# Deeper weight buffers for the last tile, gate stores on another queue, S5 outputs grouped by array tile

## The chip, the cores and the metric

The kernel runs as one program on one core of a Trainium2 chip. The metric is the device time of one execution in microseconds (us). Three runs of the kernel before took 1943.7, 1947.05 and 1947.4 us; the median, 1947.05, is the figure to compare with.

## The reference, cut to what matters

One layer for two groups of tokens: 512 prompt tokens, and 8 samples of 8 tokens. An S5 state-space mixer and an RWKV-7 mixer share one input projection; their outputs go through `w_out`, and then a product-key expert layer (PEER) follows: per token and head the 16 best of 128 x 128 experts.

```python
y = einsum(c_re, hs_re) - einsum(c_im, hs_im) + d_skip * u      # S5 outputs
x = x + ga1 * (concat([y_s5, y_rw]) @ w_out)
h = rmsnorm(x, norm2_g) * (1 + sc2) + sh2
q = (h @ w_q).reshape(T, 8, 2, 64)
s1, s2 = q[:, :, 0] @ keys1, q[:, :, 1] @ keys2                  # then top 16 of the pair sums
act = gelu(sum(u_tab[idx] * h))
ff = sum(gate * act * v_tab[idx])
y = rmsnorm(x + ga2 * ff, final_norm_g)
```

## The kernel before, in words

The 576 tokens are five tiles, taken in `ORDER = (1, 2, 3, 0, 4)`: tile 0 holds the 64 sample tokens, tiles 1 to 4 the prompt, 128 tokens each. Tiles 1, 2 and 3 are "dense": for them the expert layer runs as two full matrix products over all 16384 experts, in 128 blocks of 128 experts, with a table of gates that is zero for the experts not chosen. Tiles 0 and 4 gather their chosen rows instead.

**First part.** `phase1` makes the input projection; beside it `s5gen` computes the S5 group. Its outputs (lines 755 to 771) come for 4 quarters of 8 groups: per pair of groups `j` four matmuls of 64 rows (state against `CL`, real and imaginary part, the two halves `hf` of the array each into its own PSUM bank `pts[hf]`), and then two matmuls of 128 rows (`U` against `Tm`) that finish the pair's sums.

**Tile pipeline.** Five steps are woven, step `i` holding at most: `back` of the next tile and `front` of the one after (RWKV), `select` of tile `od[i]`, `pick` of tile `od[i-1]`, and `gbuild` of tile `od[i-2]`.
- `select` multiplies by `w_out` (line 1229, eight 512 KB loads `wo`), applies the modulation rows `ga`, `sh` and a norm, turns the result `h2` (line 1246) into `hT` (line 1257), multiplies by `w_q` (line 1269, eight 512 KB loads `wq`, one per head) and scores against `keys` (lines 1283 and 1285). All those loads go through one pool with two buffers (`tag="w", bufs=2`).
- `pick` finds the top 16 on VectorE, and for a dense tile leaves the chosen indices and gates in `dib` and `dix` (lines 1381 and 1382).
- `gbuild` makes the gate table of one dense tile in 32 groups of 4 tokens: VectorE makes a one-hot `oh` (line 1487); ScalarE (lines 1491, 1492) or VectorE (line 1494) makes `B`; ScalarE (line 1497) or GpSimd (line 1499) makes `A`; TensorE multiplies (line 1502); ScalarE copies into `Gst` (line 1503); every fourth group a 1 MB store `Gd<-Gst` leaves on SyncE's queue (line 1505). The tiles `ab` of `A` and `B` come from 9 buffers for the first two dense tiles, and for the third (`d == 2`) from a second pool `gp2` with 15.

In the last step (`i = 4`) only `select` of tile 4, `pick` of tile 0 and `gbuild` of tile 3 are left. `SO = {4: 4000}` gives that `select` a higher priority.

**Dense loop.** After the last `select`, 128 blocks: load 512 KB of `u_t` and of `v_tab`, split each into two parts (ScalarE line 1513, VectorE line 1514; lines 1615, 1616), first product `pd` (line 1517, 24 matmuls), Gelu, times the gates `Gr` (loaded back from `Gd` for 8 blocks at a time, line 1572), second product `po` (line 1620, 18 matmuls). `pick` of tile 4 and the 384 gathers of tiles 0 and 4 run beside it.

A scheduler orders each engine's instructions from a priority and a model of times; the order is fixed when the program is built. Every load or store of SyncE and ScalarE takes one of eight completion semaphores in turn, and its issue waits until the earlier transfer on that semaphore has landed.

Of the kernel before, what the change touches and what calls it, by code (L numbers as in the profile page):

```python
# [6 lines left out]
F32 = mybir.dt.float32  # L7
# [11 lines left out]
D = 1024  # L19
# [3 lines left out]
KB = 8  # L23
# [154 lines left out]
class Kernel:  # L178
# [4 lines left out]
    RATE = 3.0  # L183
    WS5, WAD, WS6, WA6, WD = 3.0, 0.0, 1.0, 1.0, 0.3
    PB = {"r": 3, "s": 3, "h": 1, "g": 1}
    UX, UWT, AB2 = 0, 0.5, 15
    UG = True
    UO = -100000
    PO, GO, SO, RO, FO = {}, {}, {4: 4000}, {}, {}
    FB = 32  # L190
    PW = 3.0
    B2 = {"r": 7, "l": 8, "b": 7, "s": 5}
# [451 lines left out]
    def s5gen(self, A):  # L644
        nc, I, O, vc, ident, p3 = self.nc, self.I, self.O, self.vc, self.ident, self.p5
        V, S, G, T, SY = nc.vector, nc.scalar, nc.gpsimd, nc.tensor, nc.sync
# [6 lines left out]
        U = p3.tile([128, 32, 72], F32, name="U", tag="U")  # L653
# [7 lines left out]
        for q in range(4):  # L661
            for r in range(2):
                pt = ps([128, 4, 72])
                for jj in range(4):
                    j = 4 * q + jj
# [20 lines left out]
        Tm = self.pB.tile([128, 32, 128], F32, name="Tm", tag="BTm")  # L686
# [72 lines left out]
        for q in range(4):  # L759
            pts = [ps([72, 4, 128]), ps([72, 4, 128])]  # L760
            for jj in range(4):
                j = 4 * q + jj
                for r in range(2):
                    for hf in range(2):
                        sl = slice(64 * hf, 64 * hf + 64)
                        T.matmul(pts[hf][:, jj, :], Hs[sl, r, j, 0:72], CL[sl, r, j, 1:9, :].rearrange("p a b -> p (a b)"),
                                 start=(r == 0), stop=False)
                for hf in range(2):
                    T.matmul(pts[hf][:, jj, :], U[:, 2 * j + hf, :], Tm[:, 2 * j + hf, :], start=False, stop=True)
            for hf in range(2):  # L770
                S.activation(Y[:, :, 8 * q + hf:8 * q + 8:2, :], pts[hf].rearrange("p g (t h) -> p t g h", h=16), AF.Gelu)
            yield
# [52 lines left out]
    def open_outer(self):  # L825
        o = self.so = Scope(self.tc)
        kw = dict(side="right", reuse_waits="tile")
        self.sm = o.pool("sm", 2, **kw)
        dn = o.pool("dn", **kw)
        self.dix = dn.tile([128, 2, 128 * len(self.DENSE)], F32, name="dix")  # L830
        io = dn.tile([128, 160], F32, name="iota")
        self.nc.sync.dma_start(io, self.I["iota"])
        self.dib = dn.tile([128, 128 * len(self.DENSE)], BF16, name="dib")
        self.io4 = dn.tile([128, 128, 4], BF16, name="io4")
        self.nc.gpsimd.tensor_copy(self.io4, io[:, :128, None].to_broadcast([128, 128, 4]))
        self.iota, self.off, self.wid = io[:, :128], io[:, 128:144], io[:, 144:160]
        m = self.sx = Scope(self.tc)
        wq = m.pool("wq", **kw)
        self.ws = m.pool("ws", **kw)
        self.t2p["s"] = m.pool("t2s", **kw)  # L840
        self.t4p["s"] = m.pool("t4s", **kw)
        self.sw = m.pool("sw", 1, **kw)
        self.G2 = wq.tile([128, D], F32, name="G2")
        g = self.sg = Scope(self.tc)
        self.gp = g.pool("gp", **kw)
        self.gs = g.pool("gs", self.GS, **kw)
# [354 lines left out]
    def select(self, ti):  # L1201
        yo = self.yo.pop(ti)
        nc, I, O = self.nc, self.I, self.O
        V, S, G, T, SY = nc.vector, nc.scalar, nc.gpsimd, nc.tensor, nc.sync
        t2, t4, ps, ident, sm = self.t2, self.t4, self.ps, self.ident, self.sm
        sw = self.sw
        smp = ti == 0
        dns = ti in self.DENSE
        c0 = 0 if smp else 64 + 128 * (ti - 1)
        ysd = t2([4, 128], "s")  # L1210
        if smp:
            SY.dma_start(ysd[:, :, 0:64], self.yd[:, :, 0:64])
            SY.dma_start(ysd[:, :, 64:128], self.yd[:, :, 0:64])
        else:
            SY.dma_start(ysd, self.yd[:, :, c0:c0 + 128])
        x1 = t4([D], "s")
        if smp:
            SY.dma_start(x1[0:64], I["x_all"][0:64, :])
            SY.dma_start(x1[64:128], I["x_all"][0:64, :])
        else:  # L1220
            SY.dma_start(x1, I["x_all"][c0:c0 + 128, :])
        tmp = t4([D], "s")
        lhs = [ysd[:, k, :] if k < 4 else yo[:, k - 4, :] for k in range(KB)]
        pos_ = [ps([128, 512], "s"), ps([128, 512], "s")]
        for k in range(KB):
            wo = self.ws.tile([128, D], F32, name="wo", tag="w", bufs=2)
            SY.dma_start(wo, I["w_out"][k * 128:(k + 1) * 128, :])
            for n in range(2):
                T.matmul(pos_[n], lhs[k], wo[:, n * 512:(n + 1) * 512], start=(k == 0), stop=(k == KB - 1))  # L1229
            if k % 2:  # L1230
                yield
        ga1 = self.ws.tile([128, D], F32, name="ga1", tag="w", bufs=2)
        self.mod(ga1, 0, smp)
        sh2 = self.ws.tile([128, D], F32, name="sh2", tag="w", bufs=2)
        self.mod(sh2, 1, smp)
        for n in range(2):
            V.tensor_tensor(tmp[:, n * 512:(n + 1) * 512], pos_[n], ga1[:, n * 512:(n + 1) * 512], op=OP.mult)
        V.tensor_tensor(x1, x1, tmp, op=OP.add)
        ss = sm.tile([128, 1], F32, name="ss")
        S.activation(tmp, x1, AF.Square, accum_out=ss)  # L1240
        self.rstd(ss, ss, 1e-6, 128, sm)
        SY.dma_start(self.x1d[ti], x1)
        yield
        h2 = t4([D], "s")
        V.scalar_tensor_tensor(h2, x1, ss, self.G2, op0=OP.mult, op1=OP.mult)
        V.tensor_tensor(h2, h2, sh2, op=OP.add)
        self.tap("h2%d" % ti, h2)
        yield
        if not dns:
            SY.dma_start(self.h2d[ti], h2)  # L1250
        hT = t4([KB, 128], "s")
        for q in range(2):
            pt = ps([128, 4, 128], "s")
            for k in range(4):
                T.transpose(pt[:, k, :], h2[:, (4 * q + k) * 128:(4 * q + k + 1) * 128], ident)
            qs = slice(4 * q, 4 * q + 4)
            S.copy(hT[:, qs, :], pt)
            yield
        if dns:
            SY.dma_start(self.h2d[ti], hT.rearrange("p k t -> p (k t)"))  # L1260
        qT = t4([8, 128], "s")
        for q in range(2):
            pt = ps([128, 4, 128], "s")
            for hh in range(4):
                h = 4 * q + hh
                wq = self.ws.tile([128, KB, 128], F32, name="wq", tag="w", bufs=2)
                SY.dma_start(wq, I["w_q"][h])
                for k in range(KB):
                    T.matmul(pt[:, hh, :], wq[:, k, :], hT[:, k, :], start=(k == 0), stop=(k == KB - 1))  # L1269
                yield  # L1270
            S.copy(qT[:, 4 * q:4 * q + 4, :], pt)
        keys = self.ws.tile([128, 8, 128], F32, name="keys", tag="w", bufs=2)
        self.kld = SY.dma_start(keys, I["keys"])
        sc4 = []
        for g0 in range(0, 4 if smp else 8, 4):
            for sd in range(2):
                sl = slice(64 * sd, 64 * sd + 64)
                pt = ps([128, 4, 128], "s")
                for u in range(4):
                    if smp:  # L1280
                        for hf in range(2):
                            r = slice(64 * hf, 64 * hf + 64)
                            T.matmul(pt[r, u, :], qT[sl, 4 * hf + u, r], keys[sl, 4 * hf + u, :], start=True, stop=True)
                    else:
                        T.matmul(pt[:, u, :], qT[sl, g0 + u, :], keys[sl, g0 + u, :], start=True, stop=True)
                s = t2([4, 128], "s")
                S.copy(s, pt)
                sc4.append((g0, sd, s))
                yield
        self.sc4[ti] = sc4  # L1290
# [181 lines left out]
    def gbuild(self, d):  # L1472
        V, S, G, T, SY = self.nc.vector, self.nc.scalar, self.nc.gpsimd, self.nc.tensor, self.nc.sync
        iob = self.iota[:, None, :].to_broadcast([128, 4, 128])
        n = self.TG
        gp, nb = (self.gp2, self.AB2) if d == 2 and self.AB2 else (self.gp, self.AB)
        for tg in range(128 // n):
            Gst = self.gs.tile([128, 128, n], F32, name="Gst")
            for q in range(n // 4):
# [22 lines left out]
                    T.matmul(pg[:, t, :], B[:, t, :], A[:, t, :], start=True, stop=True)  # L1502
                S.copy(Gst[:, :, 4 * q:4 * q + 4], pg.rearrange("p t n -> p n t"))
                yield
            SY.dma_start(self.Gd[d * (128 // n) + tg], Gst.rearrange("p n t -> p (n t)"))

    def ublock(self, b, pa, pool):
        nc, dh, dl = self.nc, self.dh, self.dl
# [10 lines left out]
    def open_dense(self):  # L1519
# [11 lines left out]
        self.hf = self.sh.pool("hf", **kw).tile([128, KB, N], F32, name="hf")  # L1531
        if self.AB2:
            self.gp2 = self.sh.pool("gp2", **kw)
        ua = self.sh.pool("ua", **kw)
        self.ua = []
        for b in range(self.UX):
            t = ua.tile([128, KB, 128], F32, name="ua%d" % b)
            SY.dma_start(t, self.I["u_t"][b])
            self.ua.append(t)
        self.dh = dq.tile([128, KB, N], F32R, name="dh")  # L1540
        self.dl = dq.tile([128, KB, N], F32R, name="dl")
        self.wu = []
# [193 lines left out]
```

## Time and profile before

| what | value |
|---|---|
| median of three runs | 1947.05 us |
| the profiled execution: its time / its span | 1942.16 / 1940.4 us |
| TensorE busy | 1813.4 us, 93% |
| VectorE, ScalarE, GpSimd busy | 79%, 42%, 35% |
| first matmul of the dense loop | 829.61 us |
| last quarter of S5 outputs ends | 211.79 us |

Engines are PE (TensorE), PEld (its weight loads), DVE (VectorE), ACT (ScalarE), POOL (GpSimd) and SP (SyncE); L1502 is line 1502 of the kernel before. An idle time before an instruction is shown in brackets with what ended it. A matmul in 4-byte numbers appears as two records, so 18 matmuls of an order listing can stand as 36 in the profile; those of the dense loop appear once.

### The profile page before, as it was taken

To read this page: it belongs to the slowest core of one execution; us is meant where nothing else is said; L and a number is where in the kernel's file an instruction comes from. 1 tells how busy PE (TensorE), PEld (TensorE's weight loads), DVE (VectorE), ACT (ScalarE), POOL (GpSimd) and SP (SyncE) were. 2 spreads that over 40 slices of the span, in tenths; PEclk is the share of its full clock that TensorE was granted. 3 is DMA by queue.
4 is the path that set the end of the run, shared out by engine and by line. 5 is a ranking of instruction groups with operands and counts; after the bars stand their busy time and mean duration, and the time that the engine had idled before them with its cause. 6 is when DMAs were issued, how large, how long until landed. Compare 5 with 4: busy or idle time off the path is not lost.

```text
span 1940.4 us, 30575 instructions
## 1 busy us (share of the span) xinstructions
PE 1813.4 (93%) x11183; PEld 1568.4 (81%) x11183; DVE 1534.4 (79%) x3117; ACT 816.9 (42%) x1494; POOL 679.7 (35%) x543
## 2 busy tenths in 40 slices
PE   8899998999979888689999999999999999999993
PEld 5699566777759686679999988899899999999992
DVE  7968335478797979299988877798888878888998
ACT  4222515535764788434333333433333333333332
POOL 0000201001252244313455433355445444444555
PEclk9899999989999999899999999999999999999997
DMA  9424653434345576789899998899999999999985
GB/s 332 150 86 104 215 186 104 146 129 152 116 168 181 191 267 241 283 281 311 301 372 353 351 354 315 274 380 348 345 356 318 344 340 345 330 340 352 328 312 198
DMA packets 203366, 514.09 MB, mean 265 GB/s; under 512 B 26248, under 2 KB 88840, under 8 KB 199120
## 3 DMA queue, kind: packets, MB, share of 16 engines
q1 hardware_dynamic: 147632, 309.74, 46.0%
q0 software_dynamic: 55584, 202.40, 28.6%
q8 instruction: 88, 1.44, 0.3%
q14 instruction: 62, 0.51, 0.1%
HBM read 471.28 MB, written 39.62 MB: 263 GB/s over the span
## 4 chain that ended last, share of the span: by engine, by line
PE 68%; DVE 14%; ACT 5%; issue 5%; DMA 5%; POOL 3%; SPq 0%; POOLq 0%; DVEq 0%; ACTq 0%
PE po L1620 23%; PE pd L1517 23%; PE par L329 5%; POOL gr L1445 3%; PE pas L1269 2%; PE par L1026 2%; DMA wq<-w_q 2%; PE par L1034 1%; PE pag L303 1%; PE pas L1229 1%; PE par L1038 1%; DVE oh L1487 1%; DMA gr<-v_tab,ei 1%; DVE ab L1494 1%; DVE idxu L1306 1%
## 5 line engine op out<-in xcount | busy, mean ns | idle before, releaser
L1445 POOL DMA_INDIRECT gr<-u_tab,ei x192 | 249.1, 1297 | 307.2 <-DVE scr L1450 255.5
L1445 POOL DMA_INDIRECT gr<-v_tab,ei x192 | 256.8, 1338 | 275.1 <-DVE acc L1460 241.7
L1517 PE MATMUL pd<-dh,uh 128*128 128x384 f32 x1024 | 344.7, 337 | 4.2 <-ACT wf L1598 2.9
L1517 PE MATMUL pd<-dh,ul 128*128 128x384 f32 x1024 | 344.9, 337 | 2.1 <-DVE ul L1514 2.1
L1517 PE MATMUL pd<-dl,uh 128*128 128x384 f32 x1024 | 343.7, 336 | 0.0
L1460 DVE SCALAR_TENSOR_TENSOR acc<-gr,act,acc 128x1024 f32<-128x1024 f32 x190 | 245.5, 1292 | 4.4 <-DMA gr<-v_tab,ei 2.7
L1513 ACT CAST uh<-ur 128x1024 fp32r<-128x1024 f32 x128 | 134.4, 1050 | 269.0 <-PE pd L1517 265.0
L1620 PE MATMUL po<-vl,wh 128*128 128x512 f32 x768 | 237.3, 391 | 2.0 <-DVE vl L1616 2.0
L1620 PE MATMUL po<-vh,wl 128*128 128x512 f32 x768 | 236.6, 390 | 0.0
L1450 DVE SCALAR_TENSOR_TENSOR scr<-gr,h 128x1024 bf16<-128x1024 f32 x192 | 234.2, 1220 | 2.3 <-DMA gr<-u_tab,ei 1.2
L1603 ACT CAST wh<-wf 128x384 fp32r<-128x384 f32 x128 | 65.8, 514 | 335.9 <-PE po L1620 311.9
L1514 DVE TENSOR_TENSOR ul<-ur,uh 128x1024 fp32r<-128x1024 f32 x128 | 156.5, 1223 | 61.8 <-ACT uh L1513 59.7
L1620 PE MATMUL po<-vh,wh 128*128 128x512 f32 x768 | 200.3, 396 | 4.9 <-ACT vh L1615 4.4
L1517 PEld LDWEIGHTS pd<-dh,uh 128*128 128x128 f32 x1024 | 192.8, 188 | 12.4 <-ACT wf L1598 4.8
L1517 PEld LDWEIGHTS pd<-dl,uh 128*128 128x128 f32 x1024 | 192.7, 188 | 5.2
L1517 PEld LDWEIGHTS pd<-dh,ul 128*128 128x128 f32 x1024 | 192.7, 188 | 3.4 <-DVE ul L1514 3.2
L1616 DVE TENSOR_TENSOR vl<-vr,vh 128x1024 fp32r<-128x1024 f32 x128 | 156.4, 1222 | 18.7 <-ACT vh L1615 15.1
L1620 PEld LDWEIGHTS po<-vl,wh 128*128 128x128 f32 x768 | 143.8, 188 | 33.3 <-DVE vl L1616 2.9
L1620 PEld LDWEIGHTS po<-vh,wl 128*128 128x128 f32 x768 | 144.1, 188 | 31.5 <-DVE wl L1604 0.3
L1620 PEld LDWEIGHTS po<-vh,wh 128*128 128x128 f32 x768 | 141.0, 188 | 33.4 <-ACT vh L1615 10.0
L1615 ACT CAST vh<-vr 128x1024 fp32r<-128x1024 f32 x128 | 134.5, 1051 | 42.5 <-PE po L1620 34.8
L1499 POOL TENSOR_TENSOR ab<-oh,dix 128x512 f32<-128x512 bf16 x72 | 87.6, 1221 | 150.6 <-DVE oh L1487 69.5
(472 smaller groups left out, 3134.8 us busy)
## 6 DMA issues: line engine op xcount, KB each, us to landing
ur<-u_t SPq DMA_DIRECT2D x128, 512.0 KB
vr<-v_tab SPq DMA_DIRECT2D x128, 512.0 KB
Gd<-Gst SPq DMA_DIRECT2D x24, 1024.0 KB
Gr<-Gd SPq DMA_DIRECT2D x16, 1536.0 KB
wo<-w_out SPq DMA_DIRECT2D x40, 512.0 KB
wq<-w_q SPq DMA_DIRECT2D x40, 512.0 KB
wt<-w_ada SPq DMA_DIRECT2D x32, 512.0 KB
wr<-w_in SPq DMA_DIRECT2D x18, 512.0 KB
```

Source lines behind the costliest of these rows:

```text
L329: mm = self.nc.tensor.matmul(p, w[:, k, :], h[:, k, c:c + 288], start=(k == 0 and i == 0), stop=(k == KB - 1 and i == 2))
L1445: G.indirect_dma_start(out=r, out_offset=None, in_=I[tab], in_offset=bass.IndirectOffsetOnAxis(ap=ei[:, k:k + 1], axis=0))
L1450: V.scalar_tensor_tensor(scr, r, 1.0, h2, op0=OP.mult, op1=OP.mult, accum_out=act[:, k:k + 1])
L1460: V.scalar_tensor_tensor(acc, r, act[:, k:k + 1], acc, op0=OP.mult, op1=OP.add)
L1499: G.tensor_tensor(A, oh, bc(self.dix[:, 1]), op=OP.mult)
L1513: nc.scalar.copy(uh, ur)
L1514: self.mark = nc.vector.tensor_tensor(ul, ur, uh.bitcast(F32), op=OP.subtract).ins
L1517: nc.tensor.matmul(pa, u[:, k, :], h[:, k, :], start=(k == 0 and i == 0), stop=(k == KB - 1 and i == 2))
L1603: S.copy(wh, wf)
L1615: S.copy(vh, vr)
L1616: V.tensor_tensor(vl, vr, vh.bitcast(F32), op=OP.subtract)
L1620: T.matmul(outs[2 * d + n], w[:, d * 128:(d + 1) * 128], v[:, n * 512:(n + 1) * 512], start=(b == 0 and i == 0), stop=(b == 127 and i == 2))
```

## The change

The last tile's `select` takes its weights from a new pool `w4` with eight buffers. It lies where `gp2` was, so the third gate table now shares the 9 buffers of the first two (`AB2 = 0`). `SO` is empty: the last `select` has no raised priority. The gate stores are issued by ScalarE instead of SyncE. In the S5 outputs a quarter's 16 matmuls of 64 rows come first and its 8 of 128 rows after them. Lines from 767 on stand 2 or 3 further down in the new file.

```diff
-    UX, UWT, AB2 = 0, 0.5, 15
+    UX, UWT, AB2 = 0, 0.5, 0
-    PO, GO, SO, RO, FO = {}, {}, {4: 4000}, {}, {}
+    PO, GO, SO, RO, FO = {}, {}, {}, {}, {}
...
                         T.matmul(pts[hf][:, jj, :], Hs[sl, r, j, 0:72], CL[sl, r, j, 1:9, :].rearrange("p a b -> p (a b)"),
-                                 start=(r == 0), stop=False)
+                                 start=(r == 0 and jj == 0), stop=False, skip_group_check=True)
+            for jj in range(4):
+                j = 4 * q + jj
                 for hf in range(2):
-                    T.matmul(pts[hf][:, jj, :], U[:, 2 * j + hf, :], Tm[:, 2 * j + hf, :], start=False, stop=True)
+                    T.matmul(pts[hf][:, jj, :], U[:, 2 * j + hf, :], Tm[:, 2 * j + hf, :], start=False, stop=True,
+                             skip_group_check=True)
...
-        self.ws = m.pool("ws", **kw)
+        self.ws, self.wsb = m.pool("ws", **kw), 2
...
-            wo = self.ws.tile([128, D], F32, name="wo", tag="w", bufs=2)
+            wo = self.ws.tile([128, D], F32, name="wo", tag="w", bufs=self.wsb)
...
-                wq = self.ws.tile([128, KB, 128], F32, name="wq", tag="w", bufs=2)
+                wq = self.ws.tile([128, KB, 128], F32, name="wq", tag="w", bufs=self.wsb)
...
-            SY.dma_start(self.Gd[d * (128 // n) + tg], Gst.rearrange("p n t -> p (n t)"))
+            S.dma_start(self.Gd[d * (128 // n) + tg], Gst.rearrange("p n t -> p (n t)"))
...
-        ua = self.sh.pool("ua", **kw)
-        self.ua = []
-        for b in range(self.UX):
...
+        self.ws, self.wsb = self.sh.pool("w4", **kw), 8
```

How the order moves, at three places. First TensorE in `s5gen`, one quarter of the S5 outputs (`pas` is the PSUM bank, `Hs` and `CL` feed the 64-row matmuls, `U` and `Tm` the 128-row ones), as a difference:

```order
-L766 MATMUL pas<-CL,Hs 72x128 x2
-L769 MATMUL pas<-Tm,U 72x128 x2
-L766 MATMUL pas<-CL,Hs 72x128 x4
-L769 MATMUL pas<-Tm,U 72x128 x2
+L766 MATMUL pas<-CL,Hs 72x128 x14
+L771 MATMUL pas<-Tm,U 72x128 x8
```

The short alternating runs became one run of each kind. In the second and third quarter the two halves come one after the other (runs of 8 in one bank); in the first and the fourth they alternate. Next SyncE's queue at the last tile's loads, before:

```order
L1267 DMA wq<-w_q 128x1024 x2
L1221 DMA t4s<-x_all 128x1024
L1505 DMA Gd<-Gst 128x2048
L1273 DMA keys<-keys 128x1024
L1227 DMA wo<-w_out 128x1024
L1505 DMA Gd<-Gst 128x2048
L1227 DMA wo<-w_out 128x1024
L1215 DMA t2s<-yd 128x4x128
```

and now:

```order
L1270 DMA wq<-w_q 128x1024 x2
L1230 DMA wo<-w_out 128x1024
L1224 DMA t4s<-x_all 128x1024
L1230 DMA wo<-w_out 128x1024 x7
L1276 DMA keys<-keys 128x1024
L1218 DMA t2s<-yd 128x4x128
L820 DMA ga_7379<-modd 128x1024
L820 DMA sh_7381<-modd 128x1024
L1270 DMA wq<-w_q 128x1024 x7
L1245 DMA x1d<-t4s 128x1024
```

The `keys` here are still those of tile 0: the last tile's eight `wo` now stand ahead of them, and seven of its `wq` ahead of its `x1d` store. Last TensorE ahead of the dense loop, from the transposes of tile 4's `h2` (`con,t4s`) on, before:

```order
L1255 MATMUL pas<-con,t4s 128x128 x8
L1502 MATMUL par<-ab 128x128 x4
L1502 MATMUL pah<-ab 128x128 x4
L1502 MATMUL par<-ab 128x128 x8
L1269 MATMUL pas<-t4s,wq 128x128 x16
L1502 MATMUL par<-ab 128x128 x4
L1502 MATMUL pag<-ab 128x128 x4
L1502 MATMUL pah<-ab 128x128 x4
L1269 MATMUL pas<-t4s,wq 128x128 x48
L1285 MATMUL pas<-keys,t4s 128x128 x16
L1517 MATMUL pd<-dh,uh 128x384
```

and now:

```order
L1258 MATMUL pas<-con,t4s 128x128 x8
L1505 MATMUL par<-ab 128x128 x8
L1505 MATMUL pag<-ab 128x128 x4
L1505 MATMUL par<-ab 128x128
L1272 MATMUL pas<-t4s,wq 128x128 x56
L1505 MATMUL par<-ab 128x128 x3
L1272 MATMUL pas<-t4s,wq 128x128 x8
L1288 MATMUL pas<-keys,t4s 128x128 x4
L1505 MATMUL pah<-ab 128x128 x4
L1288 MATMUL pas<-keys,t4s 128x128 x4
L1505 MATMUL par<-ab 128x128 x4
```

Sixteen groups of four gate matmuls now stand between the first scores and the first `pd`; before, the last gate group stood ahead of six of the eight `wq` heads.

## Rows read from the trace of the kernel before

**Rows 1.** Windows: engine busy times in the first stretch of the dense loop
```profile
core 0: us, PE busy (x) PEld busy (x) DVE busy (x) ACT busy (x) POOL busy (x), PEclk, DMA share, GB/s
829.00:875.18 46.18, 41.12 (x199) 36.33 (x200) 46.18 (x192) 17.06 (x25) 10.00 (x8) 0.96 0.80 278
```
**Rows 2.** Chain that ended last, dense loop: start, length, what
```profile
875.18 4.12 PE po L1620 x18
879.30 4.18 PE pd L1517 x24
```
**Rows 3.** Timeline of PE, last tile's select: start, length, what, idle before
```profile
795.43 3.74 PE L1269 MATMUL pas<-t4s,wq 128*128 128x128 f32 x32
...
818.45 5.20 PE L1269 MATMUL pas<-t4s,wq 128*128 128x128 f32 x32 [4.39 <-DMA wq<-w_q]
...
829.61 0.45 PE L1517 MATMUL pd<-dh,uh 128*128 128x384 f32 x1 [1.15 <-ACT t2s L1287]
```
**Rows 4.** Waits of PE from 700 to 830: total, times, longest
```profile
PE pas L1269 <- DMA wq<-w_q: 8.7, 4, 4.4
```
**Rows 5.** Waits of SyncE's queue from 700 to 830
```profile
SPq L1505 <- ACT Gst L1503: 32.6, 10, 6.5
```
**Rows 6.** Timeline of SyncE's queue, last step
```profile
709.45 6.89 SPq L1267 DMA_DIRECT2D wq<-w_q  x2
...
721.38 0.33 SPq L1273 DMA_DIRECT2D keys<-keys  x1
...
802.49 0.33 SPq L1505 DMA_DIRECT2D Gd<-Gst  x1
```
**Rows 7.** Timeline of ACT: indices of tile 3 ready, hT of tile 4 copied
```profile
730.05 0.30 ACT L1381 CAST dib<-pas 128x128 bf16<-128x128 f32 x1
...
793.61 1.08 ACT L1257 COPY t4s<-pas 128x512 f32<-128x512 f32 x2
```
**Rows 8.** Groups of DVE, 727 to 796: busy, mean ns, idle before
```profile
L1487 DVE TENSOR_TENSOR oh<-io,dib 128x512 bf16<-128x512 bf16 x33 | 15.1, 473 | 4.0 <-POOL ab L1499 4.0
L1494 DVE TENSOR_TENSOR ab<-iota,dix 128x512 f32<-128x512 f32 x16 | 13.5, 842 | 0.0
```
**Rows 9.** Windows: all engines from 727 to 796, and from 780 to 800
```profile
727.00:796.00 69.00, 53.50 (x341) 43.48 (x332) 61.19 (x191) 60.22 (x163) 30.85 (x27) 0.90 0.63 236
780.00:800.00 20.00, 14.34 (x105) 14.17 (x106) 10.96 (x18) 17.21 (x44) 7.73 (x7) 0.74 0.58 220
```
**Rows 10.** Groups of ACT, 727 to 804: busy, mean ns, idle before
```profile
L1491 ACT ACTIVATE ab<-iota,dix 128x128 f32<-128x128 f32 x68 | 22.0, 405 | 0.0
L1503 ACT COPY Gst<-par 128x512 f32<-128x512 f32 x20 | 11.3, 582 | 2.9 <-PE par L1502 1.6 <-DMA Gd<-Gst 1.3
L1497 ACT ACTIVATE ab<-oh,dix 128x128 f32<-128x128 bf16 x34 | 11.3, 411 | 6.9 <-DVE oh L1487 6.9
L1492 ACT ACTIVATE ab<-ab 128x512 f32<-128x512 f32 x17 | 11.0, 645 | 0.0
```
**Rows 11.** Timeline of DVE: h2 of tile 4, and its first scores
```profile
788.80 2.07 DVE L1246 TENSOR_TENSOR t4s<-t4s,sh 128x1024 f32<-128x1024 f32 x1
...
827.28 0.87 DVE L1305 MAX8 vals<-t2s 128x8 f32<-128x128 f32 x4 [33.51 <-ACT t2s L1287]
```
**Rows 12.** Timeline of POOL: a load that waited for the last gate store
```profile
807.81 0.78 POOL L1441 DMA_DIRECT2D h<-h2d  x1 [12.85 <-DMA Gd<-Gst]
```
**Rows 13.** Chain that ended last, S5 outputs: start, length, what
```profile
187.26 0.37 PE pas L766 x4
...
188.22 0.59 PE pas L766 x8
...
191.75 0.79 PE par L329 x6
192.55 0.58 PE pas L766 x4
193.13 0.37 PE pas L769 x2
```

More of the change, by code (lines that the diff above doesn't have):

```diff
@@ L1231, in select @@
                 yield
-        ga1 = self.ws.tile([128, D], F32, name="ga1", tag="w", bufs=2)
+        ga1 = self.ws.tile([128, D], F32, name="ga1", tag="w", bufs=self.wsb)
         self.mod(ga1, 0, smp)
-        sh2 = self.ws.tile([128, D], F32, name="sh2", tag="w", bufs=2)
+        sh2 = self.ws.tile([128, D], F32, name="sh2", tag="w", bufs=self.wsb)
         self.mod(sh2, 1, smp)
@@ L1271, in select @@
             S.copy(qT[:, 4 * q:4 * q + 4, :], pt)
-        keys = self.ws.tile([128, 8, 128], F32, name="keys", tag="w", bufs=2)
+        keys = self.ws.tile([128, 8, 128], F32, name="keys", tag="w", bufs=self.wsb)
         self.kld = SY.dma_start(keys, I["keys"])
@@ L1533, in open_dense @@
             self.gp2 = self.sh.pool("gp2", **kw)
-        ua = self.sh.pool("ua", **kw)
-        self.ua = []
-        for b in range(self.UX):
-            t = ua.tile([128, KB, 128], F32, name="ua%d" % b)
-            SY.dma_start(t, self.I["u_t"][b])
-            self.ua.append(t)
+        self.ws, self.wsb = self.sh.pool("w4", **kw), 8
         self.dh = dq.tile([128, KB, N], F32R, name="dh")
```

## The prediction, made before the result was known

> **What bounds the kernel now.** I read the windows of the dense loop first, then the chain that ended last, then TensorE's timeline and waits ahead of the loop, and last the queues and the groups of VectorE and ScalarE between 700 and 830 us. The reader should see three different limits.
>
> *The dense loop is TensorE's.* One block costs 4.12 + 4.18 = 8.30 us in the chain [rows 2], and 128 blocks are 1062 us. The change touches no matmul of it. What it can move is when the loop starts (first `pd` at 829.61 [rows 3]) and how well it starts: by 875.18 five `pd` and four `po` are done, 5 x 4.18 + 4 x 4.12 = 37.4 us of work, while 45.6 us have passed [rows 1, 2]. The ramp thus loses about 8 us.
>
> *The step before the loop is a chain over several engines.* Tile 3's chosen indices are ready at 730.05 and `hT` of tile 4 is copied by 793.61 + 1.08 = 794.7 [rows 7]; the `wq` product, the scores and the first `pd` follow, 829.61 - 794.7 = 34.9 us later [rows 3]. In the first piece VectorE is busy 61.2 of 69.0 us [rows 9], so it is the bound there; 15.1 us of it are one-hots `oh` and 13.5 us are `B` tiles [rows 8], which only fill the time of `h2` (ready at 788.80 + 2.07 = 790.9 [rows 11]) and are not needed for it. In the second piece VectorE is idle for 33.5 us [rows 11], and TensorE waits 8.7 us for `wq` in four waits, the longest 4.39 [rows 3, 4].
>
> *SyncE's queue is blocked, not busy.* It stood 32.6 us in ten waits at the `Gd` stores, each for a `Gst` copy [rows 5]; a `wq` or `wo` load behind such a store can't be issued.
>
> The S5 part is TensorE's too: the chain runs from 187.26 to the end of the last quarter at 211.79 on TensorE alone, 24.5 us [rows 13].
>
> **The sum.** It is made against the profiled execution, 1942.16 us, which is 4.9 us under the median 1947.05; that difference is added at the end.
>
> 1. *S5 outputs.* Two 128-row records take 0.37 and four 64-row ones of one half take 0.58 [rows 13], so a record costs (0.58 - 0.37) / 2 = 0.105 us and a change of tile shape 0.37 - 0.21 = 0.16. Eight 64-row records of alternating halves take 0.59 [rows 13], that is 0.054 each: the halves run side by side. Before, the chain has some 46 short runs there. Now there are 12: 64 records of 128 rows x 0.105 = 6.7 us, 64 of 64 rows in the second and third quarter, where the halves are not alternated, x 0.105 = 6.7, 64 alternated ones x 0.054 = 3.5, and 12 x 0.16 = 1.9; 18.8 us in all. Of the 24.5 us, 0.8 is other work between the runs [rows 13], so 4.9 us are saved. I take **-4.5**; the ends are -5.2 (34 changes x 0.16 fewer) and 0, if TensorE then only waits longer for weights that are still loading.
>
> 2. *`keys` of tile 0, later.* Before, they were issued at 721.38, five us after the last `wq` of that tile (709.45 + 6.89 = 716.3) [rows 6]. Now eight `wo` of the last tile and one load of `x_all` stand ahead of them. That is 4.2 + 0.5 MB, with their own 0.5 MB 5.2 MB; the rate of the first stretch of the loop, 278 GB/s [rows 1], makes 18.7 us of it, its rate at full share, 278 / 0.80, makes 15. So `keys` land at some 731 to 735, where before some 725 is my estimate (issue, 2 us of bytes and as much of latency). TensorE takes its instructions in order, so tile 0's scores hold up tile 3's index transposes behind them: **+8**, from 0 (if the burst spreads) to +10.
>
> 3. *`hT` sooner.* In the new order about 13 of the `oh` and 5 or 6 of the `B` tiles of VectorE have moved behind `h2`, because the third table has 9 `ab` buffers instead of 15 and the last `select` starts with its weights there. VectorE is the bound [rows 9]: 13 x 0.473 + 5.5 x 0.842 [rows 8] = **-10.7**, ends -6 (if the 7.8 us that VectorE has free grow) and -12.
>
> 4. *`hT` to the first `pd`.* Before, 34.9 us, of which 8.7 are waits for `wq` [rows 4]; those loads are now early, so these waits go. But the gate work did not vanish, it moved here: sixteen groups stand between the first scores and `pd`. Behind `hT`, ScalarE now has 20 `Gst` copies x 0.57 = 11.4, six sets of four of line 1491 at 4 x 0.324 = 1.3 make 7.8, four sets of line 1497 at 4 x 0.332 make 5.3, seven of line 1492 x 0.645 make 4.5 (busy time over count [rows 10]), six copies of `qT` and scores of about 0.57 make 3.4, three casts of about the 1.08 of [rows 7] 3.2, and five store issues x 0.33 [rows 6] 1.7: 37 us. TensorE has 128 records of `wq` (3.74 per 32 [rows 3], 15.0 us) ahead of the gate groups that ScalarE waits for; of that I count 2.5 to 4. Together 39.5 to 41, against 34.9: **+5**. Ends: -4 (31 us, the same sets overlapped throughout) and +10.
>
> 5. *The ramp.* `pick` of tile 4 and the first casts overlap the gate tail now, so more blocks are ready when `pd` starts: **-3** of the 8 us lost, ends 0 and -4. What may be late next is `Gr`: it can load only after the last store, which before landed 5.3 us after its issue (802.49 to 807.81 [rows 6, 12]). It is needed after the first `pd`; I count it as hidden by three of them, 3 x 4.18 = 12.5 us. If that cover is gone, up to 8 us are lost.
>
> 6. *Stores moved in the first two tables.* Sixteen issues of 0.33 us on ScalarE, which has slack there, and as many fewer on SyncE: **0**, +/-3. ScalarE is the engine that makes `Gst`, so a store waits for nothing else, but it can wait for a completion semaphore, and then the next `Gst` copy is queued behind it, with TensorE's gate groups behind that.
>
> Sum: -4.5 + 8 - 10.7 + 5 - 3 + 0 = **-5.2**, so 1937.0 for the profiled execution and about **1941** with the 4.9 of the median.
>
> **A rule against the trace.** Ten waits of 32.6 us [rows 5] against ten issues of 0.33 [rows 6] show that at these stores the queue's cost was waiting, not issuing. The Trainium skill (DMA: Bandwidth & Descriptors, section "Issuing engines are not separate DMA queues") says that all engines' transfers run on the same 16 DMA engines, and that issuing from several saves only the sequencer's time to issue; by it the move of ten stores would be worth 10 x 0.33 = 3.3 us of SyncE's time at most, none of it on the path. The trace disagrees in part, since the loads behind those stores were held by order. It does bear on term 2: the bytes stay the same, and bringing loads forward makes other loads late. That is the third rival.
>
> **Rivals.**
>
> - *A, slower: the gate tail on ScalarE ends the step.* Its place is between `hT` and the first `pd`. If the gate groups wait for all 15.0 us of `wq` records and nothing overlaps, the piece lasts 37.3 + 15.0 = 52.3 us, 17.4 more than before instead of 5. The sum is then +7.2, the time **1954**. It decides from 40 + 5.2 = 45 us on. For it: ScalarE is already busy 17.2 of the 20 us from 780 to 800, and TensorE's granted clock there is 0.74 on the mean of a scale where 1.2 GHz is 0.5 and 2.4 GHz is 1 [rows 9], so the gate matmuls run partly at the lower level. Against it: ScalarE had 60.2 busy of 69 us [rows 9] and yet waited only 6.9 us for `oh` and 2.9 around `Gst` [rows 10], that is, it is fed well when the buffers are there.
> - *B, much faster:* `keys` are not late (0 for +8) and the tail overlaps (-4 for +5). Then -4.5 - 10.7 - 4 - 3 = -22.2, or **1925**. For it: 0.63 is the mean DMA share in the last step [rows 9], so there is room. Against: the wo burst comes at one moment.
> - *C, no change: the gains come out as waits elsewhere.* The S5 time saved turns into a wait for the weights of the modulation that follow (0 for -4.5), and the moved stores only save their issue. Then the sum is about -1, the time **1946**. For it: many loads share the 16 DMA engines there. Against: the S5 chain has no idle time in front of it [rows 13].
>
> **How the numbers follow.** A measurement of this kernel can tell about 0.2%, 3.9 us, from no change: faster is below 1943.2, slower above 1950.9. The forecast case (some 1937 to 1943) has 0.35, B 0.20, C 0.23, A 0.22. Faster is forecast and B, 0.55; same is C, 0.23; slower is A, 0.22. The range of 8 in 10 goes to the middle of B and of A, 1925 to 1954, which leaves half of each, 0.21, outside. The forecast case's own range is 1936 to 1944.
>
> **What would show it.** S5: the quarter's runs in 12 pieces, its end 4 to 5 us sooner after its start than 24.5 us; if TensorE then waits behind it, C. `keys`: the wait of tile 0's scores for that load, longer than before, and `dib` of tile 3 copied about 8 us later than 730.05. `h2` of tile 4 some 50 us after that copy instead of 61. No waits of TensorE for `wq`; after `hT`, waits for `par` and `Gst` on ScalarE in their place, and a first `pd` about 40 us after the copy of `hT`. SyncE no longer waits at any `Gd` store. The loop at 8.30 us per block. I am wrong if the first `pd` comes later than 829.61 plus what S5 saves, if ScalarE waits long at store issues, if the loop loses time over `Gr`, or if the blocks themselves change.

## The result, and the profile after

The changed kernel takes 1957.15 us (median of 11 runs, 1950.97 to 1966.28) against 1947.05; the ratio is 1.0059, 95% interval 1.0045 to 1.0074. It is **slower by 10 to 12 us** (10.1 between the medians, 11.5 by the ratio), where 1941 was forecast, and it lies above the range of 1925 to 1954. A second set of runs beside the kernel before gave 1.0059 again (1.0040 to 1.0078).

Its profiled execution has a span of 1949.2 us against 1940.4, but it was the fastest of its eleven runs; most of the reason is told with the last experiments. The marks of its last step, ScalarE first (start, length, instruction, idle before): chosen indices of tiles 2 and 3, and `hT` of tile 4.

```profile
627.77 0.28 ACT L1384 CAST dib<-pas 128x128 bf16<-128x128 f32 x1
...
739.36 0.31 ACT L1384 CAST dib<-pas 128x128 bf16<-128x128 f32 x1
...
786.43 1.05 ACT L1260 COPY t4s<-pas 128x512 f32<-128x512 f32 x2
```

These answer to [rows 7], where the second was at 730.05 and the third at 793.61. The first, not shown there, was at 633.03. TensorE in the same stretch, with tile 0's scores, the `wq` product and the first `pd` (before: [rows 3]):

```profile
735.81 1.59 PE L1286 MATMUL pas<-keys,t4s 64*64 64x128 f32 x32 [0.72 <-DMA keys<-keys]
...
790.55 12.67 PE L1272 MATMUL pas<-t4s,wq 128*128 128x128 f32 x112
...
832.28 0.42 PE L1520 MATMUL pd<-dh,uh 128*128 128x384 f32 x1
```

The `wq` product runs without a wait now, 112 records in one piece, as the change intends. Yet `pd` comes at 832.28, later than 829.61. SyncE's queue shows the two orders that the change brought, against [rows 6]: `keys` behind eight `wo`, and `Gr` last.

```profile
712.37 0.65 SPq L1230 DMA_DIRECT2D wo<-w_out  x1
...
713.95 8.45 SPq L1230 DMA_DIRECT2D wo<-w_out  x7
723.98 0.33 SPq L1276 DMA_DIRECT2D keys<-keys  x1
...
837.13 4.69 SPq L1570 DMA_DIRECT2D Gr<-Gd  x2
```

The chain of the last step (start, length, what) goes through both: the issue of `keys` waits for a `wo` load, and tile 0's scores wait for `keys`.

```profile
713.95 9.97 DMA wo<-w_out
723.98 11.79 DMA keys<-keys
735.81 1.59 PE pas L1286 x32
```

In the windows view the DMA engines are at a busy share of 0.98 while `keys` are on their way, over 24 us:

```profile
core 0: us, PE busy (x) PEld busy (x) DVE busy (x) ACT busy (x) POOL busy (x), PEclk, DMA share, GB/s
712.00:736.00 24.00, 17.68 (x124) 16.83 (x124) 7.07 (x13) 15.06 (x40) 7.55 (x6) 0.79 0.98 367
```

The chain that ended last (start, length, what), behind the last gate group, and one wait of VectorE between 826 and 875 (total, times, longest):

```profile
832.56 0.60 ACT Gst L1506
833.18 3.87 DMA Gd<-Gst
837.13 14.54 DMA Gr<-Gd
851.72 0.40 issue
852.11 0.56 DVE wf L1598
```

```profile
DVE wf L1598 <- DMA Gr<-Gd: 6.5, 1, 6.5
```

How the loop stands is counted from its records up to a time: windows of `pd` alone, then of `po` alone, from 0 to 874 us and from 0 to 1880 us, of the kernel before

```profile
0.00:874.00 874.00, 27.66 (x139) 0.96 0.54 185
0.00:1880.00 1880.00, 553.49 (x3024) 0.98 0.75 267
...
0.00:874.00 874.00, 13.58 (x54) 0.96 0.54 185
0.00:1880.00 1880.00, 531.14 (x2212) 0.98 0.75 267
```

and of the changed one:

```profile
0.00:874.00 874.00, 23.41 (x118) 0.95 0.53 181
0.00:1880.00 1880.00, 545.75 (x2990) 0.98 0.75 266
...
0.00:874.00 874.00, 10.70 (x36) 0.95 0.53 181
0.00:1880.00 1880.00, 525.22 (x2178) 0.98 0.75 266
```

24 records of `pd` are 4.18 us and 18 of `po` 4.12 [rows 2]. Before, the work done by 874 is 139 x 4.18 / 24 + 54 x 4.12 / 18 = 36.6 us, as if the loop had begun at 837.4; now it is 28.8, a begin at 845.2. I call that the counted start. One table holds the rest of the story; every value is a difference of such rows:

| kernel | dib tile 2 to dib tile 3 | dib tile 3 to first pd | first pd to counted start | counted start to end |
|---|---|---|---|---|
| before | 97.0 | 99.6 | 7.8 | 1103.0 |
| changed | 111.6 | 92.9 | 12.9 | 1104.0 |
| changed, again | 111.2 | 92.9 | 13.0 | 1105.1 |
| Gr from elsewhere (after_nogr) | 110.1 | 92.5 | 7.9 | 1099.3 |
| gates raised (after_go) | 110.9 | 84.1 | 13.9 | 1103.7 |
| keys first (after_kf) | 97.9 | 92.4 | 13.4 | 1103.0 |
| both (after_kfgo) | 98.8 | 82.7 | 16.0 | 1101.7 |
| both, again (kfgo_b) | 99.0 | 84.1 | 15.9 | 1101.1 |
| two buffers (after_w2) | 98.4 | 101.6 | 11.9 | 1101.7 |
| two buffers, gates raised (w2_go) | 98.7 | 99.7 | 8.3 | 1099.8 |

The first column holds the wait for `keys`, the second `hT` and the gate tail, the third the ramp, the last the loop and what follows it. The change loses 14.6 us in the first column, gains 6.7 in the second, loses 5.1 in the third, and 1.0 in the last.

### The profile page after: what moved, and what is told of

The parts are those of the page before. It is cut to its first block, busy times and chain, and to the rows that moved or that the text cites. A ratio compares the mean times of both kernels' runs of the same rounds, so it can differ in the third digit from the quotient of the medians.

```text
span 1949.2 us, 30572 instructions
## 1 busy us (share of the span) xinstructions
PE 1817.6 (93%) x11183; PEld 1575.6 (81%) x11183; DVE 1534.6 (79%) x3117; ACT 817.7 (42%) x1494; POOL 688.6 (35%) x543
## 4 chain that ended last, share of the span: by engine, by line
PE 72%; DVE 14%; DMA 6%; ACT 5%; issue 2%; SPq 0%; POOL 0%; ACTq 0%; DVEq 0%; POOLq 0%
PE pd L1520 26%; PE po L1618 26%; PE par L329 5%; PE pas L1272 2%; PE par L1029 2%; PE par L1037 1%; DVE oh L1490 1%; PE pag L303 1%; PE par L1041 1%; DVE ab L1497 1%; PE pas L1232 1%; DMA wo<-w_out 1%; DVE idxu L1312 1%; PE pas L792 1%; DMA Gr<-Gd 1%
## 5 line engine op out<-in xcount | busy, mean ns | idle before, releaser
L1448 POOL DMA_INDIRECT gr<-v_tab,ei x192 | 263.2, 1371 | 270.8 <-DVE acc L1463 236.7
L1520 PEld LDWEIGHTS pd<-dh,uh 128*128 128x128 f32 x1024 | 192.7, 188 | 11.7 <-ACT wf L1596 5.8
```

What stands on the lines that cost most here:

```text
L1448: G.indirect_dma_start(out=r, out_offset=None, in_=I[tab], in_offset=bass.IndirectOffsetOnAxis(ap=ei[:, k:k + 1], axis=0))
L1520: nc.tensor.matmul(pa, u[:, k, :], h[:, k, :], start=(k == 0 and i == 0), stop=(k == KB - 1 and i == 2))
```

## The experiments

**One part alone.** Four runs share their runs of the kernel before. The first has only the S5 grouping of the diff ahead of the prediction.

> The kernel before with the S5 outputs grouped and nothing else. My theory: the changed kernel's loss sits in the last step before the dense loop (late keys, gate groups behind the last select, gate table loaded late), and the S5 grouping keeps its 4.9 us; so about 5 us faster than before (ratio 0.9970 to 0.9985), the S5 chain some 19.7 us long, the first pd about 5 us sooner. Rival (the gain becomes a wait for other work behind S5): within 2 us of before.

Measured: 1941.8 us, ratio 0.9984 (0.9968 to 1.0000): 3 us, with an interval that ends at no change. The chain of the matmuls is shorter as forecast, but the first `pd` is at 832.38, not 5 us sooner than 829.61. The profile shows where time goes back. ScalarE at the end of the S5 outputs, with the grouping alone and then in the kernel before:

```profile
206.89 0.59 ACT L774 ACTIVATE Y<-pas 72x512 f32<-72x512 f32 x1 [2.33 <-PE pas L771]
212.93 0.31 ACT L924 ACTIVATE gs<-t 128x128 f32<-128x128 f32 x1 [5.45 <-DMA t<-pd]
213.14 1.06 ACT L774 ACTIVATE Y<-pas 72x512 f32<-72x512 f32 x2
```

```profile
210.04 0.31 ACT L921 ACTIVATE gs<-t 128x128 f32<-128x128 f32 x1 [2.34 <-DMA t<-pd]
211.60 1.08 ACT L771 ACTIVATE Y<-pas 72x512 f32<-72x512 f32 x2 [1.25 <-PE pas L769]
```

Before, the last two outputs `Y` waited for TensorE; now they stand behind `gs`, which waits for a load. TensorE then waits for the transposed result of `Y`, 2.57 us where it was 0.78 before, and its granted clock falls (timeline, then two windows of the kernel with the grouping alone):

```profile
217.56 0.47 PE L781 MATMUL pas<-con,Y 72*128 72x72 f32 x4 [2.57 <-DVE y L783]
```

```profile
216.00:218.00 2.00, 0.44 (x5) 0.44 (x6) 1.51 (x2) 2.00 (x7) 0.88 (x1) 1.00 0.98 391
220.00:222.00 2.00, 2.00 (x10) 0.67 (x7) 0.00 (x0) 1.99 (x4) 1.56 (x2) 0.50 0.00 0
```

TensorE had 0.44 us of work between 216 and 218 us; between 220 and 222 it is busy throughout at a granted clock of 0.50, the 1.2 GHz level. The kernel before shows 1.00 from 216 to 224. In the five profiles without the grouping the first `wo` matmul comes 90.6 to 92.3 us after the last S5 matmul; in the twelve with it, 93.0 to 96.6. So most of the 4.9 us is gone by there; that the wait for `Y` and the clock are all of it was not tested by a run.

The second has only the stores moved:

```diff
-            SY.dma_start(self.Gd[d * (128 // n) + tg], Gst.rearrange("p n t -> p (n t)"))
+            S.dma_start(self.Gd[d * (128 // n) + tg], Gst.rearrange("p n t -> p (n t)"))
```

> The kernel before with the gate stores issued by ScalarE and nothing else. My theory: the place of issue by itself costs or gives little, 0 +/- 3 us (ratio 0.9985 to 1.0015). Rival (the stores hold up ScalarE, whose Gst copies and gate tiles are queued behind them): slower by 5 to 10 us, with waits of ScalarE at its stores.

Measured: 1948.1 us, ratio 1.0007 (0.9994 to 1.0020). The rival falls: no loss of 5 us.

The third takes the eight buffers away from the changed kernel:

```diff
-        self.ws, self.wsb = self.sh.pool("w4", **kw), 8
+        pass
```

> The changed kernel without the pool of eight buffers: the last select again takes its weights through two; S5 grouping, stores on ScalarE and the third set of 9 buffers stay. No gate group stands behind the first scores here, and keys of tile 0 are issued ahead of all wo. My theory (eight buffers make keys late and let the select overtake the gates): the loss goes, 1938 to 1944 or 13 to 19 us below the changed kernel (ratio to before 0.995 to 0.999), keys landed some 5 us after their issue, Gr not waited for. Rival (the 9 buffers or the stores make the loss): still 1952 or more.

Measured: 1946.9 us, ratio 1.0005 (0.9993 to 1.0017). Ten microseconds of the loss go with the pool, and the first column of the table is back at 98.4. No gain is left, though: the second column is 101.6, 8.7 above the changed kernel, and the time does not reach the forecast 1938 to 1944.

The fourth raises the priority of the third gate table in the changed kernel:

```diff
-    PO, GO, SO, RO, FO = {}, {}, {}, {}, {}
+    PO, GO, SO, RO, FO = {}, {4: 4000}, {}, {}, {}
```

> The changed kernel with a raised priority for the third gate table: eight buffers stay and keys are still behind eight wo, but the gate groups stand between the wq matmuls, none behind the first scores, and Gr is issued ahead of most loads of the blocks. My theory splits the loss in two: keys late by 9 to 10 us stays, the tail and the late Gr (2.7 + 4.4 us) go, so 1947 to 1952 (ratio 1.000 to 1.003). Rival (late keys are all of it): as the changed kernel, 1955 to 1960. Rival (the order inside the loop is all of it): as the changed kernel as well, with the first block on time.

Measured: 1947.0 us, ratio 1.0008 (0.9997 to 1.0019), 10 us below the changed kernel. The time is at the lower end of the forecast, but by the profile not for both reasons given. `keys` are as late as in the changed kernel (110.9 in the table), and the second column falls by 8.8. The ramp stays at 13.9, although VectorE has no wait for `Gr` in it: there TensorE waits for `ul`, one of the two parts of the split `u_t` (waits from 805 to 875 us).

```profile
PE pd L1520 <- DVE ul L1517: 4.3, 2, 2.4
```

**The three suspects apart.** The first two `Gr` loads read other rows in one kernel:

```diff
+            src = self.Gd[:, :, g * GBL * TG:(g + 1) * GBL * TG].rearrange("g p x -> p g x") if g > 1 else \
+                I["v_tab"][0:3072, 128 * g:128 * g + 128].rearrange("(g p) x -> p g x", p=128)
```

> The changed kernel, but the first two loads of Gr (gates of the first 16 blocks) read rows of v_tab of the same size and pattern in place of Gd, so they wait for no store; the gates of those blocks are not the reference's. TensorE's order ahead of the first pd is the same as in the changed kernel. Theory (the loop starts without its gates because the last store comes behind the gate tail): the wait of the first blocks goes, 4 to 7 us less than the changed kernel, 1950 to 1953, loop started by about 840 instead of 845 when counted back from 870 us. Rival (the wait for Gr is hidden and the tail alone counts): 1955 or more.

Measured: 1947.9 us, ratio 1.0011 (0.9996 to 1.0026), 9 us below. In the profile the first two columns stay within 1.5 us and the third falls from 12.9 to 7.9, the value of before: in the changed kernel the ramp's extra 5 us hang on `Gr`. The edit also moves the two loads forward in SyncE's queue, to 804.62 and 817.91 us. The last column is 4.7 shorter as well; it is 1099.3 to 1105.1 in the ten profiles of the table, so a part of the 9 us may be that scatter.

Another issues the last `wo` loads after tile 0's `keys`:

```diff
+            if self.wsb == 8:
+                with self.tc.issue_after(self.kld.ins):
+                    SY.dma_start(wo, I["w_out"][k * 128:(k + 1) * 128, :])
```

> The changed kernel with the wo loads of the last select issued after the keys load of tile 0; eight buffers and the gate tail stay. Theory (late keys hold up the third gate table, so everything behind it, the tail and Gr): tile 0's scores some 10 us sooner, first pd and Gr 6 to 10 us sooner, 1947 to 1951 (ratio 1.000 to 1.003). Rival (the raised priority run already showed that only the place of the gates counts, late keys do not): 1954 to 1958.

Measured: 1941.5 us, ratio 0.9973 (0.9955 to 0.9991), faster than the kernel before. SyncE's queue and TensorE's scores of tile 0 in that kernel:

```profile
716.43 0.33 SPq L1280 DMA_DIRECT2D keys<-keys  x1
716.80 6.65 SPq L1232 DMA_DIRECT2D wo<-w_out  x8
```

```profile
721.55 1.59 PE L1290 MATMUL pas<-keys,t4s 64*64 64x128 f32 x32
```

The scores start 5.1 us after the issue of `keys`, where the changed kernel needed 11.8, and 14.3 us sooner. Of the columns the first moves, from 111.6 to 97.9, and the others by 1 us at most: late keys cost 13.7 us by the profile. The rival, that they do not count, falls. From 712 to 736 us this kernel moves 373 GB/s, no less than the 367 of the changed one: it is the place behind the `wo` loads that made `keys` late, not a fuller window.

Both together:

> The changed kernel with both: wo after keys, and a raised priority for the third gate table. Theory (two separate losses of the change, late keys and the late gate table): both go, and the gain of the early weights is left, first pd near 820, 1936 to 1942 (ratio 0.995 to 0.998). Rival (what ends the step without the tail is something else, such as ScalarE's gate work): as with the raised priority alone, 1945 to 1949.

Measured: 1930.65 us, ratio 0.9918 (0.9903 to 0.9934), below the range that I had given (a second set of runs, further down, lies in it). The two gains add up in the first two columns (98.8 and 82.7), but the ramp is 16.0. The next wait is TensorE's, behind the first `pd`, and it comes from a `vr` load that now stands behind `Gr` (timelines of TensorE and ScalarE):

```profile
809.02 0.44 PE L1524 MATMUL pd<-dh,uh 128*128 128x384 f32 x1
...
825.39 0.69 PE L1524 MATMUL pd<-dh,uh 128*128 128x384 f32 x1 [11.94 <-ACT wf L1600]
```

```profile
822.49 1.04 ACT L1617 CAST vh<-vr 128x1024 fp32r<-128x1024 f32 x1 [6.12 <-DMA vr<-v_tab]
```

The smaller third set, with the stores moved as above, on the kernel before:

```diff
-    UX, UWT, AB2 = 0, 0.5, 15
+    UX, UWT, AB2 = 0, 0.5, 0
```

> The kernel before with the third gate set on the 9 buffers of the first two and the gate stores on ScalarE; no S5 grouping, no eight buffers, the select's raised priority stays. Beside the run without the eight buffers this tells what the smaller set costs and what S5 gives. Theory (the smaller set costs some us, which ate the S5 gain of 3 us there): slower than before by 3 to 5 us (ratio 1.0015 to 1.0025). Rival (the smaller set costs nothing): within 2 us of before.

Measured: 1949.9 us, ratio 1.0020 (1.0004 to 1.0035), as the theory had it; it is 2 us more than with the stores alone, but the intervals overlap, so a cost of the smaller set by itself is not shown. Its ramp is 11.7 us, with no wait for `Gr`.

**What the parts are worth in the better version.** The changed kernel with gates raised, and the pool of eight taken out as above:

> The changed kernel with the raised priority of the third gate table and without the eight buffers, two as before. It tells whether the early weights are what the best version gains from. Theory (the eight buffers are worth over 10 us once keys and gates are not late): 1943 to 1948, waits of TensorE for wq back. Rival (the raised priority and the other parts give the gain): 1929 to 1936.

Measured: 1940.5 us, ratio 0.9996 (0.9979 to 1.0012). This is below the range that the theory gave in microseconds, but its runs of before were lower too (1944.4). Beside 0.9918 and, later, 0.9946, it says that the eight buffers are worth 0.5 to 0.8% where their two costs are gone: the second column is 99.7 without them and 82.7 to 84.1 with them. TensorE's waits for `wq` are back, 9.7 us in three.

From the version with both edits, the stores back on SyncE (the store's line as before):

> The version with wo after keys and the raised priority of the third gate table, but the gate stores issued by SyncE again; TensorE's order ahead of the loop is the same. Theory (loads behind a store on SyncE wait for its Gst copy, so the move of the stores matters once the loads are early): SyncE waits some 20 to 35 us at the stores again, first pd 3 to 10 us later than 809, 1934 to 1942. Rival (the place of issue saves only the issuing): 1929 to 1933, as with ScalarE.

The same without the S5 grouping (those lines as before):

> The version with wo after keys and the raised priority, without the S5 grouping. Theory (of the 4.9 us that the grouping saves on TensorE, some 3 come through, since ScalarE's last S5 outputs then stand behind a load): 1932 to 1935, 2 to 4 us above the version with it. Rival (nothing comes through): within 1 us of it. Rival (all of it): 5 us above.

Measured: 1935.4 us, 0.9962 (0.9947 to 0.9976), and 1935.6 us, 0.9956 (0.9939 to 0.9973). Each median is 5 us above 1930.65, which was measured on another chip, while their profiles show no such loss in the last step: from tile 2's `dib` to the first `pd` it is 181.8 and 181.2 us, and 181.5 with both edits. So all three ran again, side by side:

> The version with wo after keys and the raised priority once more, on the same chip as the two that undo one part of it. Theory: ratio 0.990 to 0.994 as in its first run, first pd 181 to 182 us after the first dib copy of that stretch (tile 2's, at about 630). Rival (its five runs were lucky ones): 0.994 to 0.997, like the two with a part undone.

> The same with the stores on SyncE, once more. Its first profile had 25 us of waits of SyncE at the stores and yet the same 181.8 us from tile 2's dib copy to the first pd as with ScalarE (181.5), so in the last step the place of issue gave nothing. Theory after that (the difference of the medians came from the early part, which differs from run to run): within 0.2% of the version with ScalarE beside it. Rival (the stores cost time that the profiles did not show): 0.3 to 0.5% above it.

> The same without the S5 grouping, once more beside it. Theory (the grouping saves 4.9 us on TensorE, some of it lost to the wait for y and the lower clock behind it): 2 to 4 us above the version with it, 0.1 to 0.2%. Rival (nothing comes through): the same within 1 us.

Measured: 1936.75 us, 0.9946 (0.9926 to 0.9966); stores on SyncE 1938.9, 0.9949 (0.9930 to 0.9968); no grouping 1936.9, 0.9946 (0.9926 to 0.9966). My theory for the grouping falls: nothing that can be measured comes through. Nor do the stores tell: 2 us between the medians, which the intervals can't separate, although SyncE waited there for 25.1 us, where [rows 5] has 32.6 (waits of the first run with the stores on SyncE, 700 to 830 us):

```profile
SPq L1512 <- ACT Gst L1510: 25.1, 10, 9.1
```

The 0.9918 of the version with both edits stood on five runs; nine more say 0.9946, as the rival (lucky ones) had it, and the first `pd` comes 183.1 us after tile 2's `dib`, outside the 181 to 182 that I gave. The version is faster than the kernel before by 0.5 to 0.8%.

**The changed kernel again.**

> The changed kernel once more, beside the same runs of the kernel before as the three others: its first profile was its fastest run, 6 us under its median. Theory (from 380 to 420 us some executions lose 5 to 6 us to a lower granted clock, whatever the kernel, and the rest of the difference is the last step): ratio 1.004 to 1.007, and in this profile the span from the second dib copy to the first pd is again 92 to 94 us, wherever the early part puts its start. Rival (the last step itself varies from run to run): that span differs by 4 us or more.

Measured: 1955.2 us, ratio 1.0059 (1.0040 to 1.0078); from tile 3's `dib` to the first `pd` 92.9 us, as in the first profile. What differs is an early stretch of the same program, first profile and second (windows, columns as above):

```profile
380.00:400.00 20.00, 16.91 (x204) 15.50 (x204) 12.68 (x24) 4.57 (x12) 2.58 (x4) 1.00 0.50 150
```

```profile
380.00:400.00 20.00, 16.84 (x138) 15.42 (x137) 11.38 (x22) 3.98 (x10) 2.58 (x4) 0.76 0.37 123
```

TensorE's granted clock is 1.00 in the one and 0.76 in the other, at equal busy time, and fewer records are done. From the first `wo` matmul of one tile to that of the next it took 113.3 us in the one and 117.7 in the other. The kernel before had 0.78 in that window and 117.6 us. So some 4 of the 5.3 us by which the changed kernel's first profile was ahead at tile 2's `dib` were this, not the change. In all 17 profiles this stretch takes 112.1 to 120.0 us.

## Why the prediction was wrong, point by point

Four steps failed, and one came out better than forecast. Against the sum of -5.2 the profile has about +13, once the 4 us of clock are set aside. The ramp accounts for 8.1 of the difference (term 5: the load of `Gr` itself was given no time), late `keys` for 6.6 (term 2: the bytes ahead of them), the gate tail for 4.9 (term 4), S5's way onto the path for some 3 (term 1) and the end of the loop for 1.0; `hT` gave 5.8 back (term 3).

*Term 1, S5, -4.5 forecast.* The matmuls got shorter by the amount worked out: 188.53 to 208.38 is 19.9 us, with 24.5 before (start of the chain, then TensorE's timeline, changed kernel).

```profile
188.53 1.68 PE pas L766 x28
...
206.41 1.97 PE L771 MATMUL pas<-Tm,U 128*72 128x128 f32 x16
```

The step that failed is the one from TensorE's saving to the path. With its lower end of 0 I had named a wait for weights; the profile shows a wait for ScalarE's `Y` behind a load, with a lower clock after it. Alone it measured 3 us with an interval that ends at 0, in the better version nothing.

*Term 2, keys, +8 forecast with an end of +10.* It measured +14.6 in the profile, and 13.7 of it go with one edit. The mechanism was right and the sum of bytes was wrong: I counted 5.2 MB, and the window shows 24 us at 367 GB/s, 8.8 MB. The gate stores of ScalarE, three issues of 1 MB in that window, ride beside the burst, and so does what was issued before it. The delay has two halves. Counted from tile 2's `dib`, `keys` were issued 7.9 us later than before, since the seven `wo` issues ahead of them took 8.45 us; and from issue to use they took 11.8 us instead of 4.8. Here the load queued last in a burst paid for what all queues moved meanwhile.

*Term 3, hT sooner, -10.7 forecast with an end of -12.* From tile 3's `dib` to `hT` it takes 47.1 us instead of 63.6, -16.5. The direction was right, and so was VectorE as the bound: it is busy for 46.15 of these 47.07 us. The size depends on term 2: in the run with `keys` first the piece takes 51.5 us (777.08 - 725.63), -12.1, close to the forecast end. The other 4.4 us came with the late `keys`, and term 4 paid for them.

*Term 4, hT to the first pd, +5 forecast, end +10.* 45.9 us instead of 36.0 between the starts: +9.9. That was rival A's place, a gate tail on ScalarE behind the last scores, at 57% of its +17.4. That it is the place of the gate groups is shown by the run with raised priority: the piece from `dib` to `pd` falls by 8.8 us with the same buffers. In the run with `keys` first, `hT` to `pd` takes 40.9 us, +4.9, as forecast. The other 5 us hang on term 2: late `keys` put `dib`, and with it the gate table, off by 13.7 us, but `hT` by only 9.4 (777.08 to 786.43), so more of the gate work is left for the tail.

*Term 5, the ramp, -3 forecast.* It measured +5.1, the wrong way. The prediction had the condition ("If that cover is gone, up to 8 us are lost"), but it gave a time only to the last store, 5.3 us, and none to the load of `Gr` behind it. The store took 3.87 and `Gr`, two loads of 1.5 MB, 14.54 us; three `pd` of 12.5 us did not hide 18.4. With `Gr` read from elsewhere the ramp is 7.9 us, as before. So `Gr` is the cause in the changed kernel, and not the only way to a long ramp: 13.9 with the gates raised and 11.9 with two buffers stand without a wait of VectorE for it. (In the reading of the ramp before, six `pd` and three `po` were done by 875.18, not five and four; the 37.4 us stay.)

*Term 6, the stores, 0 forecast.* Right: 1.0007 alone, and 2 us within the intervals in the better version. By the Trainium skill (DMA: Bandwidth & Descriptors, section "Issuing engines are not separate DMA queues") the move saves only the issuing time. The runs agree, since 25 us of waits at the stores went with no measurable loss: the waits of [rows 5], which I had held against that rule, cost nothing that can be measured.

The sum by the profile: 14.6 - 6.7 + 5.1 + 1.0 = 14.0, less the 5.3 by which it was ahead at tile 2's `dib`, is 8.7 of the 8.8 us. Since some 4 of those 5.3 were the clock of one execution, about 13 is what the profile gives to the change; the times have 10 to 12. The 1 to 3 us between them are not explained; an S5 gain of 3 us in place of the 1 us of this profile would cover most of them. The prediction's own slips were small beside this: 34 changes at 0.16 us are 5.4, not 5.2, and 1937.0 + 4.9 is nearer to 1942 than to 1941.

*The loop itself* was forecast unchanged. By the count at 1880 us the changed kernel has a start of 860.7 (520.8 + 498.5 us of work), 13.7 later than before (847.0 by the same count), after 7.8 at 874. Some 6 us more than before were lost on the way, nearly all of it between 1200 and 1300 us. They hardly show in the time: what follows 1880 us is shorter by 4.9, 3.1 of it behind the last `po`, and from counted start to end the two differ by 1.0 us. A loss inside a loop has to be followed to the end before it is booked.

*The rivals.* None was right as told. C's guess that the S5 gain turns into a wait came true, though for another load; A had the place and the sign; the late keys and late `Gr`, both named in the terms, carried the rest. What I had not done is add the bad ends of terms that hang together: a select that overtakes the gates makes keys late, the tail long and `Gr` late at once. Their bad ends (+10, +10 and 0 with up to 8 lost) give -4.5 + 10 - 10.7 + 10 + 8 = +12.8, or 1960.

What stays open: how much of the 9 us with `Gr` from elsewhere lies outside the ramp; what makes the ramp long where VectorE does not wait for `Gr`; what the removed priority of the last `select` does by itself, which no run has alone; and whether `vr` ahead of `Gr` would take the 11.94 us wait of the better version, which was not tried.

## What to carry to other kernels

More buffers move loads forward, and what is moved forward moves something else back: look up what each queue now issues late, and give that load's landing the bytes of all queues in that stretch. Give every transfer of a chain a time of its own, the load behind the last store too. Costs that come from one cause (here a step that overtakes another) are added at their bad ends together, not one by one at their means. Where extra buffers disappoint, keep them and repair the order: here two small edits turned +0.6% into -0.5 to -0.8%.

## What was not expected of the hardware

The same program lost about 4 us in one stretch in one execution and not in another, with a granted clock of 0.76 against 1.00 there, so one profile against one profile carries an error of that size, and its marks must be compared from a common point. And a store on ScalarE waited for a load of SyncE: in the changed kernel ScalarE stood idle for 4.18 us until a `wo` load had landed, and the store and the instruction behind it followed. This fits the completion semaphores that the loads and stores of both engines take in turn.

```profile
725.22 0.33 ACTq L1508 DMA_DIRECT2D Gd<-Gst  x1
725.59 0.63 ACT L1495 ACTIVATE ab<-ab 128x512 f32<-128x512 f32 x1 [4.18 <-DMA wo<-w_out]
```
